# A decoder layer on one core: the low parts of the up projection's weights begin at other places in SBUF

## The chip, the cores and the metric

One core of one Trainium2 chip. The metric is the device time of one execution in microseconds, median of several runs. The kernel before takes 340.94 us (three runs, 340.84 to 341.1). Five engines work side by side on the core: TensorE (matmuls, with their weight loads as instructions of their own), VectorE, ScalarE, GpSimd and SyncE (here the issuer of all DMAs).

## The reference, cut to what matters

One hybrid decoder layer in float32 over 256 tokens of width 1024: attention and a pooling mixer side by side, gated and added to x, and then a feed-forward block. The change touches only the feed-forward block:

```python
h2 = rmsnorm(x, norm_ffn_g)
up = causal_depthwise_conv(h2 @ w_up, conv_w, conv_b)     # w_up: 1024 x 5632
gate, val = jnp.split(up, 2, axis=-1)
return x + (jax.nn.silu(gate) * val) @ w_down             # w_down: 2816 x 1024
```

## The kernel before, in words

All float32 products are made of three matmuls in the faster format float32r. Every operand is split in a high part (the value as float32r stores it) and a low part (the rest), and `mm3` adds high x high (line 94), high x low of the moving operand (line 95) and low x high (line 96). In the feed-forward block the weights are the stationary operand (128 x 128), and the activations, stored transposed, are the moving one (256 columns, all tokens). So lines 94 and 95 load the same slice of a high part, and line 96 loads the same slice of the low part.

Weights come in chunks of 128 x 2048 float32, 1 MB each, in the list `order` (lines 99 to 109): for the block, 22 up chunks and 11 down chunks, mixed. `load` (line 113) brings a chunk into one of 4 raw buffers by DMA. `next_high` (line 142) lets ScalarE write the high part into one of 4 buffers of the pool `whi`, a half chunk of 1024 columns at a time, and takes the low part's buffer from the pool `wlo` in the same breath (line 150). `next_low` (line 153) lets VectorE write raw minus high into the low buffer (line 86) and issues the next load. `ahead` runs both at places chosen by hand, so that high and low parts are ready some chunks before the matmuls need them; `chunk` (line 171) hands a chunk's two buffers to the matmuls.

One up chunk holds 1024 rows for two tiles of 128 features, one of the gate and one of the value: slices of 128 columns, 512 bytes apart per partition, 2 tiles x 8 slices (`tile_part`, line 565). So an up chunk is 48 matmuls, 16 of each line. From the fourth chunk on, each step i of the main loop (line 675) does the up tiles of chunk i and then 24 down matmuls (lines 641 to 643) for step i - 3. What else happens in a step lies on other engines: scaling and the convolution on VectorE and ScalarE, products on GpSimd. The first up tiles stand apart: between them TensorE makes the second norm's statistics (lines 242 and 253, plain float32 matmuls of another kind). After that, TensorE does nothing but up and down matmuls to the end. All instructions of one engine keep the order in which they are written (lines 709 to 715).

Where things lie in SBUF is settled by the allocator: pools follow each other in the order in which they are opened, so raw buffers, then the four of `whi`, the four of `wlo`, and behind them the activations (`act`) and temporaries. A raw, high or low buffer is 8,192 bytes in every partition, and in the program of before they all start 32 bytes past a multiple of 512. The activation tiles that are operands of the split products (`xhi`, `xlo`, `hhi`, `hlo`, `mh`, `ml`, `ath`, `poolh`, `ah`, `al` and the like) and the tiles of q and k start 480 bytes past one, with slices of 1,024 bytes; the identity matrix of the transposes starts 224 past one. Two padding lengths at the head, `HOME` and `LEAD`, set this.

Of the kernel before, what the change touches and what calls it, by code (L numbers as in the profile page):

```python
# [9 lines left out]
F32R = mybir.dt.float32r  # L10
# [4 lines left out]
P = 128  # L15
# [17 lines left out]
CH = 2048  # L33
# [21 lines left out]
FIRST = 2  # L55
HOME = 24
LEAD = 104
XCUTS = (1, 2, 3, 4, 6, 8)


@with_exitstack
def hybrid_layer_kernel(ctx: ExitStack, tc: tile.TileContext, xq_d, par_d, wkv_d, wpg_d,
# [6 lines left out]
    wlo_p = ctx.enter_context(tc.tile_pool(name="wlo", bufs=WBUFS))  # L69
# [11 lines left out]
    def high(hi, src, scale=1.0):  # L81
        nc.scalar.activation(hi, src, AF.Copy, scale=scale)  # L82
# [16 lines left out]
    order = [("q", None)] * 2 + [("k", wkv_d[c]) for c in range(2)]  # L99
# [10 lines left out]
    raws, his, los = {}, {}, {}  # L110
# [14 lines left out]
    def raw(c, sl):  # L125

        return xq[:, 4 * c + sl.start // 512, S:] if order[c][0] == "q" else raws[c][:, sl]
# [10 lines left out]
    def oldest():  # L138

        return next((c for c in range(len(order)) if c not in spent), len(order))  # L140

    def next_high():
        if at[0] < len(pieces):
            c, sl, first, _ = pieces[at[0]]
            if c - oldest() >= WBUFS:
                return
            at[0] += 1
            if first:
                his[c] = whi_p.tile([P, CH], F32R, tag="whi", name=f"hi_{order[c][0]}{c}")
                los[c] = wlo_p.tile([P, CH], F32R, tag="wlo", name=f"lo_{order[c][0]}{c}")  # L150
            high(his[c][:, sl], raw(c, sl))

    def next_low(eager=False):
# [9 lines left out]
    def ahead(upto=0):  # L163

        next_high()
        next_low()
        if at[1] - sum(p[0] < used[0] for p in pieces) < upto:
            next_high()
            next_low()
# [12 lines left out]

    xq_all = act.tile([P, LEAD + KD + KD * (S + AW)], F32, name="xq")[:, LEAD:]
    gmix = xq_all[:, 0:KD]
# [7 lines left out]
    cut = 0  # L192
    for k in XCUTS:
        end = KD + k * (S + AW)
# [28 lines left out]
    for k in range(KD):  # L223
        if k == 0:
            nc.vector.tensor_scalar(xhi[:, k, :], xT[:, k, :], gmix[:, k:k + 1], None, op0=ALU.mult)
        else:
            high(xhi[:, k, :], xT[:, k, :], gmix[:, k:k + 1])
        low(xlo[:, k, :], xhi[:, k, :], xT[:, k, :], gmix[:, k:k + 1])
        next_high()
        next_low(eager=True)  # L230
# [272 lines left out]
    for n in range(2 * KD):  # L503
# [5 lines left out]
        b, c = n // 2, n % 2  # L509
# [270 lines left out]
```

## Time and profile before

| | before |
|---|---|
| median of 3 runs | 340.94 us (340.84 to 341.1) |
| profiled execution, whole | 340.33 us |
| its span, first to last instruction | 338.6 us |
| TensorE busy, matmuls | 333.6 us (99%), 2738 matmuls |
| TensorE busy, weight loads | 323.8 us (96%) |
| VectorE, ScalarE, GpSimd busy | 259.9 (77%), 198.3 (59%), 86.4 us (26%) |
| DMA queues' share | 51.4% of 16 engines, 62.34 MB |

The views of the profile tell of one execution. Matmuls are pipelined: one takes some 0.28 us from its start to its modelled end, and the next starts long before that. So TensorE's busy time does not say how fast matmuls follow each other; the start times in the timeline do. Weight loads have rows of their own (PEld) and run beside the matmuls. "PEclk" is the share of the full TensorE clock that was granted.

### The profile page before, as it was taken

How to read it: one execution, taken by the hardware profiler on the slowest of the kernel's cores; microseconds unless marked ns; L12 is line 12 of the kernel's file. 1: busy time of each engine (PE TensorE's matmuls, PEld its weight loads, DVE VectorE, ACT ScalarE, POOL GpSimd, SP SyncE). 2: the span in 40 equal slices, each digit the busy share in tenths (PEclk: the TensorE clock that was granted, in tenths of full speed). 3: DMA queues.
4: the chain of work that ended last, by engine and by line, in shares of the span. 5: the costliest groups of instructions: out<-in, count | busy, mean ns of one | idle time of the engine just before them, and what ended most of it. 6: DMA issues, size and time to landing. Idle time of an engine off the chain costs nothing.

```text
span 338.6 us, 6730 instructions
## 1 busy us (share of the span) xinstructions
PE 333.6 (99%) x2738; PEld 323.8 (96%) x2738; DVE 259.9 (77%) x411; ACT 198.3 (59%) x319; POOL 86.4 (26%) x104
## 2 busy tenths in 40 slices
PE   8999999999999999999999999999999999999996
PEld 7888899999999999999999999999999999999995
DVE  4869989797587676798899788777777777777744
ACT  5856634635848945678366575566666665646420
POOL 1007991112203034023222322121212121212130
PEclk9999999999999999999999999999999999999999
DMA  7986562455372751466626675554646364642003
GB/s 270 417 339 240 171 222 107 156 185 206 126 271 85 248 183 71 132 251 240 250 81 197 220 250 160 215 197 178 226 149 248 126 250 137 236 149 102 0 2 124
DMA packets 10398, 62.76 MB, mean 185 GB/s; under 512 B 1152, under 2 KB 2304, under 8 KB 3456
## 3 DMA queue, kind: packets, MB, share of 16 engines
q1 hardware_dynamic: 10368, 62.34, 51.4%
q8 instruction: 21, 0.34, 0.4%
q14 instruction: 9, 0.07, 0.1%
HBM read 61.29 MB, written 1.05 MB: 184 GB/s over the span
## 4 chain that ended last, share of the span: by engine, by line
PE 97%; DMA 1%; ACT 0%; DVE 0%; issue 0%; ACTq 0%
PE ps_up L95 12%; PE ps_up L96 12%; PE ps_up L94 12%; PE ps_d L643 6%; PE ps_d L642 6%; PE ps_d L641 6%; PE ps_g L94 5%; PE ps_g L95 4%; PE ps_g L96 4%; PE ps_q L282 3%; PE ps_k L282 3%; PE ps_v L282 3%; PE ps_out L95 2%; PE ps_out L94 2%; PE ps_out L96 2%; PE ps_bp L94 1%
## 5 line engine op out<-in xcount | busy, mean ns | idle before, releaser
L94 PE MATMUL ps_up<-hhi,hi_up 128*128 128x256 f32 x352 | 97.5, 277 | 0.0
L95 PE MATMUL ps_up<-hlo,hi_up 128*128 128x256 f32 x352 | 97.3, 277 | 0.0
L96 PE MATMUL ps_up<-hhi,lo_up 128*128 128x256 f32 x352 | 97.2, 276 | 0.0
L95 PEld LDWEIGHTS ps_up<-hlo,hi_up 128*128 128x128 f32 x352 | 66.1, 188 | 0.2 <-DVE hlo L88 0.2
L94 PEld LDWEIGHTS ps_up<-hhi,hi_up 128*128 128x128 f32 x352 | 66.1, 188 | 0.0
L96 PEld LDWEIGHTS ps_up<-hhi,lo_up 128*128 128x128 f32 x352 | 66.1, 188 | 0.0
L86 DVE TENSOR_TENSOR lo_up<-raw_up,hi_up 128x1024 fp32r<-128x1024 f32 x44 | 54.8, 1247 | 6.2 <-ACT hi_up L82 6.2
L641 PE MATMUL ps_d<-ah,hi_dn 128*128 128x256 f32 x176 | 48.6, 276 | 0.0
L642 PE MATMUL ps_d<-al,hi_dn 128*128 128x256 f32 x176 | 48.6, 276 | 0.0
L643 PE MATMUL ps_d<-ah,lo_dn 128*128 128x256 f32 x176 | 48.6, 276 | 0.0
L624 POOL TENSOR_TENSOR c_v<-c_g,c_v 128x256 f32<-128x256 f32 x22 | 16.2, 737 | 118.1 <-DVE c_v L607 118.1
L82 ACT ACTIVATE hi_up<-raw_up 128x1024 fp32r<-128x1024 f32 x44 | 45.1, 1046 | 0.0
L94 PE MATMUL ps_g<-xhi,hi_g 128*128 128x256 f32 x128 | 36.4, 284 | 0.0
L82 ACT ACTIVATE ah<-c_v 128x256 fp32r<-128x256 f32 x22 | 9.2, 418 | 45.8 <-POOL c_v L624 45.8
L96 PE MATMUL ps_g<-xhi,lo_g 128*128 128x256 f32 x128 | 35.7, 279 | 0.0
L95 PE MATMUL ps_g<-xlo,hi_g 128*128 128x256 f32 x128 | 35.7, 279 | 0.0
L642 PEld LDWEIGHTS ps_d<-al,hi_dn 128*128 128x128 f32 x176 | 33.0, 188 | 0.0
L641 PEld LDWEIGHTS ps_d<-ah,hi_dn 128*128 128x128 f32 x176 | 33.0, 188 | 0.0
L643 PEld LDWEIGHTS ps_d<-ah,lo_dn 128*128 128x128 f32 x176 | 33.0, 188 | 0.0
L86 DVE TENSOR_TENSOR lo_dn<-raw_dn,hi_dn 128x1024 fp32r<-128x1024 f32 x22 | 27.3, 1242 | 0.4 <-ACT hi_dn L82 0.4
L612 DVE TENSOR_TENSOR u_v<-ps_up,R 128x256 f32<-128x256 f32 x22 | 9.3, 422 | 22.0 <-PE ps_up L96 22.0
L94 PEld LDWEIGHTS ps_g<-xhi,hi_g 128*128 128x128 f32 x128 | 24.3, 190 | 0.9 <-issue 0.5
(183 smaller groups left out, 802.3 us busy)
## 6 DMA issues: line engine op xcount, KB each, us to landing
raw_up<-in_wup SPq DMA_DIRECT2D x22, 1024.0 KB, 4.8
raw_dn<-in_wdn SPq DMA_DIRECT2D x11, 1024.0 KB, 4.8
raw_g<-in_wpg SPq DMA_DIRECT2D x8, 1024.0 KB, 4.8
raw_o<-in_wout SPq DMA_DIRECT2D x4, 1024.0 KB, 4.9
raw_v<-in_wkv SPq DMA_DIRECT2D x2, 1024.0 KB, 13.6
raw_p<-in_wpg SPq DMA_DIRECT2D x2, 1024.0 KB, 6.2
raw_bp<-in_wbp SPq DMA_DIRECT2D x2, 1024.0 KB, 4.9
raw_ba<-in_wba SPq DMA_DIRECT2D x2, 1024.0 KB, 4.8
```

The source lines that it names most:

```text
L82: nc.scalar.activation(hi, src, AF.Copy, scale=scale)
L86: nc.vector.tensor_tensor(lo, src, hi.bitcast(F32), ALU.subtract)
L94: nc.tensor.matmul(out, sh, mh, start=start, stop=False, **kw)
L95: nc.tensor.matmul(out, sh, ml, start=False, stop=False, **kw)
L96: nc.tensor.matmul(out, sl, mh, start=False, stop=stop, **kw)
L282: nc.tensor.matmul(pt[t], sx[:, k, t * P:(t + 1) * P], wx[:, sl], start=k == 0 and sx is xhi and wx is hi, stop=k == KD - 1 and wx is lo)
L612: nc.vector.tensor_tensor(u, ps[:, 0:S], R2, ALU.mult)
L624: nc.gpsimd.tensor_tensor(uc[1], g[1], uc[1], ALU.mult)
L641: nc.tensor.matmul(o, hi[:, sl], acch[i], start=first, stop=False, skip_group_check=True)
L642: nc.tensor.matmul(o, hi[:, sl], accl[i], start=False, stop=False, skip_group_check=True)
L643: nc.tensor.matmul(o, lo[:, sl], acch[i], start=False, stop=i == KF - 1, skip_group_check=True)
```

## The change

The four buffers of the pool `wlo` get 128 more columns (512 bytes). The low part of a chunk still fills 2048 columns, but for the up chunks it begins at a place that a table gives: up chunk n begins 16 x `LOWS[n]` columns, 64 x `LOWS[n]` bytes, behind the buffer's start. For all other chunks, and for up chunks whose entry is 0, it begins at the start as before. The list `at_up` in the new line counts the up chunks that stand ahead in `order`. All readers and writers of the low part get the shifted view, so that nothing else is edited.

```diff
+LOWS = (0, 0, 4, 4, 0, 2, 2, 0, 1, 1, 0, 6, 6, 0, 3, 3, 0, 5, 5, 0, 7, 7)
...
                 his[c] = whi_p.tile([P, CH], F32R, tag="whi", name=f"hi_{order[c][0]}{c}")
-                los[c] = wlo_p.tile([P, CH], F32R, tag="wlo", name=f"lo_{order[c][0]}{c}")
+                at_up = [i for i in range(c) if order[i][0] == "up"]
+                place = 16 * LOWS[len(at_up)] if order[c][0] == "up" else 0
+                los[c] = wlo_p.tile([P, CH + P], F32R, tag="wlo", name=f"lo_{order[c][0]}{c}")[:, place:]
             high(his[c][:, sl], raw(c, sl))
```

## Rows read from the trace of the kernel before

**Rows 1.** The page: busy time by engine, and the chain that ended last.
```profile
PE 333.6 (99%) x2738; PEld 323.8 (96%) x2738; DVE 259.9 (77%) x411; ACT 198.3 (59%) x319; POOL 86.4 (26%) x104
...
PE 97%; DMA 1%; ACT 0%; DVE 0%; issue 0%; ACTq 0%
```

**Rows 2.** Stretches: length, busy us (instructions) by engine, PEclk, DMA share, GB/s.
```profile
131.60:154.30 22.70, 22.70 (x196) 22.70 (x195) 17.29 (x25) 15.24 (x25) 5.46 (x8) 1.00 0.50 170
...
163.60:324.30 160.70, 160.70 (x1418) 160.67 (x1417) 124.34 (x187) 94.70 (x142) 35.87 (x42) 1.00 0.50 176
```

**Rows 3.** Timeline of TensorE: start us, duration us; four starts.
```profile
131.68 0.28 PE L94 MATMUL ps_out<-mh,hi_o 128*128 128x256 f32 x1
...
154.29 0.28 PE L94 MATMUL ps_up<-hhi,hi_up 128*128 128x256 f32 x1
...
180.15 0.28 PE L94 MATMUL ps_up<-hhi,hi_up 128*128 128x256 f32 x1
...
188.31 0.28 PE L94 MATMUL ps_up<-hhi,hi_up 128*128 128x256 f32 x1
```

**Rows 4.** Matmuls by line: count, duration ns min/median/max, first and last start.
```profile
L94 PE MATMUL ps_out<-mh,hi_o x64: 281/281/281, 131.7 to 153.9; 128*128 128x256 f32 x64
...
L95 PE MATMUL ps_up<-hlo,hi_up x10: 278/281/281, 160.0 to 163.1; 128*128 128x256 f32 x10
...
L94 PE MATMUL ps_up<-hhi,hi_up x328: 276/276/473, 163.6 to 324.0; 128*128 128x256 f32 x164
...
L641 PE MATMUL ps_d<-ah,hi_dn x176: 276/276/276, 177.4 to 334.9; 128*128 128x256 f32 x176
```

**Rows 5.** Timeline of TensorE at two disturbances, and line 95 between them.
```profile
156.41 0.28 PE L94 MATMUL ps_up<-hhi,hi_up 128*128 128x256 f32 x1
156.66 0.39 PE L95 MATMUL ps_up<-hlo,hi_up 128*128 128x256 f32 x1
...
L95 PE MATMUL ps_up<-hlo,hi_up x7: 276/276/279, 157.1 to 159.2; 128*128 128x256 f32 x7
...
163.38 0.60 PE L253 MATMUL ps_n<-diag,ones 128*128 128x256 f32 x2
163.62 0.47 PE L94 MATMUL ps_up<-hhi,hi_up 128*128 128x256 f32 x1
163.93 0.28 PE L95 MATMUL ps_up<-hlo,hi_up 128*128 128x256 f32 x1
164.05 0.28 PE L96 MATMUL ps_up<-hhi,lo_up 128*128 128x256 f32 x1
164.17 0.28 PE L94 MATMUL ps_up<-hhi,hi_up 128*128 128x256 f32 x1
```

**Rows 6.** Line 95 behind three of the 15 entries, columns as in rows 4.
```profile
L95 PE MATMUL ps_u<-xlo,hi_p x16: 276/276/280, 39.5 to 44.6; 128*128 128x256 f32 x16
...
L95 PE MATMUL ps_u<-xlo,hi_p x16: 281/281/281, 45.8 to 51.1; 128*128 128x256 f32 x16
...
L95 PE MATMUL ps_bp<-pooll,hi_bp x8: 281/281/281, 117.7 to 120.1; 128*128 128x256 f32 x8
```

**Rows 7.** Low parts from 163.6 us; a weight load in the timeline; the stage's waits.
```profile
L86 DVE TENSOR_TENSOR lo_up<-raw_up,hi_up x37: 1215/1224/1714, 162.7 to 311.0; 128x1024 fp32r<-128x1024 f32 x37
...
180.15 0.19 PEld L95 LDWEIGHTS ps_up<-hlo,hi_up 128*128 128x128 f32 x1
...
DVE u_v L612 <- PE ps_up L96: 22.0, 16, 1.7
```

**Rows 8.** Timeline of TensorE in the q projection, 512 columns; 18 matmuls apart.
```profile
11.89 0.39 PE L282 MATMUL ps_q<-lo_q,xhi 128*128 128x512 f32 x1
...
16.01 0.39 PE L282 MATMUL ps_q<-lo_q,xhi 128*128 128x512 f32 x1
```

**Rows 9.** The transposes of k: timeline, and durations of one.
```profile
54.18 1.03 PE L318 MATMUL ps_tk<-ident,qg_k 128*128 128x128 f32 x8
...
L318 PE MATMUL ps_tk<-ident,qg_k x8: 271/272/273, 54.2 to 54.9; 128*128 128x128 f32 x8
```

## The prediction, made before the change was run

> **What bounds the kernel now.** I read the page first: TensorE is busy for 333.6 us of a span of 338.6, and the chain that ended last is TensorE for 97% [rows 1]. VectorE, the next one, is at 77%. So the question for any edit here is what it does to the pace of TensorE's matmuls, and nothing else is near the path.
>
> Then the stretches of the kernel by engine [rows 2]. [...] A "busy" of 100% hides the pace, because matmuls overlap. The pace is the distance from one start to the next, and that is read from the timeline [rows 3]: between 131.68 and 154.29 us lie 192 matmuls of the output projection, 22.61 us, so 117.76 ns each; between 180.15 and 188.31 lie 72 matmuls, one whole step of up (48) and down (24), 8.16 us, so 113.33 ns each. Same shape, 128x128 weights against 256 columns, same clock, 4.43 ns apart. The duration of one matmul tells the two paces apart in the grouped views too [rows 4]: median 281 ns at the slow pace, 276 at the fast one. By that mark the up matmuls after 163.6 us, 3 x 328, and all 528 down matmuls run fast, the first of them apart; the output projection and the up matmuls from 160.0 to 163.1 run slow.
>
> The reader should see one thing more: the pace is not fixed by the operands. The same line, reading the same kind of buffers at the same distances, runs at either pace. What changes it is a disturbance of the stream [rows 5]: the matmul behind the one at 156.41 us had to wait and started 0.25 us later, and the stream that had been slow came out fast (line 95 from 157.1 to 159.2: median 276 ns); at 163.38 two matmuls of another kind cut into a slow stream, then starts follow at 0.31, 0.12 and 0.12 us, and it is fast. Between disturbances a pace is kept: the slow one through the whole output projection, the fast one for 171 us to the end. I count 15 entries into this kind of stream behind a block of other matmuls or a wait, from 39.4 to 163.6 us; 8 came out fast, 7 slow (the first two and one of the late slow ones stand in [rows 6]).
>
> **The change part by part.** No instruction is added, removed or moved, no wait either. Four buffers grow from 8,192 to 8,704 bytes. That moves what lies behind them by 2,048 bytes, a multiple of 512, so all operands but the low parts keep their places modulo 512; the buffers' own growth is 512 each. Between the two column halves of one up chunk the weights differ by 512 bytes already, and the pace is 113.33 over both in the step of [rows 3], so I put 512 at nothing. If it cost something it would do so at the slow pace's 4.43 ns.
>
> What is left is the low part of 14 of the 22 up chunks: chunks 2, 3, 5, 6, 8, 9, 11, 12, 14, 15, 17, 18, 20 and 21 begin 64 to 448 bytes further on. Call distance the start of the weights minus the start of the moving operand, modulo 512. Today it is 64 for all matmuls of the stage. In a triple of lines 94, 95, 96 it stays 64 for two, and the third gets 320, 192, 128, 448, 256, 384 and 0, two chunks each.
>
> VectorE writes these low parts (line 86, median 1,224 ns, worst 1,714 [rows 7]). If all 28 shifted ones took the worst time, 28 x 0.490 = 13.7 us more, this would go into VectorE's idle 160.7 - 124.3 = 36.4 us of the stage [rows 2]. What hides it is that VectorE works chunks ahead: it waits for up matmuls 22.0 us in 16 waits, and the waits of the stage name no matmul that waits for anything [rows 7]. So nothing; without this cover the 13.7 us would be in the sum.
>
> For TensorE no row shows the new distances with this shape. Nearest rows: at 113.33 the load of a matmul's weights starts with the matmul before it [rows 7], so weights are read while the moving operand of another matmul is, and I read the two paces as two ways in which these reads fall against each other. Distance 448 occurs with 512 columns in the q projection, weights from x and moving from the weight buffer: 18 matmuls from 11.89 to 16.01 us, 229 ns each, 114.4 per 256 columns [rows 8], between the paces. Distance 256 occurs in the transposes of k: eight take 1.03 us with the last one's 0.27, so 109 ns each [rows 9], but with 128 columns and another data path. Bounds for one shifted matmul: +4.43 ns and -4.3 ns.
>
> Now the sums, against the profiled execution, 340.33 us with a span of 338.6. Lows alone at the slow pace: 14 x 16 x 4.43 ns = 0.99 us. All matmuls of the shifted chunks: 14 x 48 x 4.43 = 2.98. If the stream is thrown to the slow pace at the first border and stays, as the slow pace stayed through [rows 3]: 20 chunks x 48 + 22 x 24 = 1,488 matmuls, 6.6 us. If nothing: 0. The sequence has 13 borders between one shift and another. I take each as a disturbance that can land either way, as 7 of 15 did, and count half of the 14 shifted steps as slow with their down matmuls: 7 x 72 x 4.43 ns = 2.23 us. That gives 342.56 for the profiled execution. The median of the three runs shown is 0.61 above the profiled one, so 343.2 us.
>
> **The rivals.** *No change.* The pace could be a matter of timing between the two streams alone and not of addresses. For it: both paces occur at one and the same distance, and the fast one passes from up to down and back at every step, with other moving tiles, without a ripple [rows 3, 4]. Against it: those tiles all sit at the same distance, so the trace never tried another. Price: 0, 340.9 us. [...]
>
> *Faster.* Some distances could read better than today's. For it: the 109 ns of the transposes. If the shifted lows went from 113.33 to 109, 14 x 16 x 4.33 ns = 0.97 us would go, 340.0; if they drew their whole triples along, 2.9 us, 338.0. Against it: in the fast pace up and down run at the same 113.33 without a trace of variation, which looks like a floor of this shape. It decides from the first shifted chunk, about 166 us.
>
> *Slower and stuck.* The same mechanism as my forecast, but no border restores the fast pace, since no matmul of another kind comes after 163.6: 6.6 us, 347.5. It decides at the first border, chunk 2.
>
> **How the numbers follow.** Slower by over 0.2% (0.68 us, about what a measurement of this kernel can tell from no change): 0.47, of which 0.05 for stuck; within 0.2%: 0.38, which holds the case of lows alone at fewer than 10 chunks; faster: 0.15. Likeliest is slower, at 343.2. Its own range is 341.7 to 347. For 8 in 10 the range takes in no change and leaves out most of the faster case and the stuck end: 340.2 to 346.8.
>
> **What would show it.** Forecast right: the up matmuls of some shifted chunks have a median of 281 ns or more and steps of about 8.48 us in place of 8.16, with TensorE still busy all the time and no new wait. If lows alone pay, only the start behind line 96 or ahead of it is late. No change: steps of 8.16 throughout. Faster: steps under 8.16 in the shifted chunks. I am wrong in kind if the time moves outside 166 to 335 us, if a wait on line 86 shows up ahead of TensorE, or if the first two chunks change.

## The result, and the profile after

| | before | after |
|---|---|---|
| median of 3 runs | 340.94 us (340.84 to 341.1) | 343.44 us (343.41 to 343.62) |
| profiled execution, whole | 340.33 us | 343.62 us |
| its span | 338.6 us | 341.8 us |
| TensorE busy, matmuls | 333.6 us | 337.5 us |

The ratio of the two is 1.0074, 95% interval 1.0051 to 1.0097: slower, by 2.5 us, and the interval leaves out no change. The forecast was 343.2.

The page of after, busy time and chain, answers to [rows 1]: the same instructions, TensorE as full as before, and nothing else moved up.

```profile
PE 337.5 (99%) x2738; PEld 327.7 (96%) x2738; DVE 259.6 (76%) x411; ACT 198.2 (58%) x319; POOL 87.4 (26%) x104
...
PE 98%; ACT 0%; DVE 0%; issue 0%; ACTq 0%
```

The waits of after from 164 us to the end, the longest and the one that answers to the wait of [rows 7] (who waited for whom, us in total, times, longest). No matmul waits for anything here either:

```profile
POOL c_v L628 <- DVE c_v L611: 119.8, 22, 6.9
...
DVE u_v L616 <- PE ps_up L98: 23.8, 16, 2.1
```

So the 3.2 us of span went into TensorE's matmuls, and nearly all of it into matmuls that follow each other more slowly. The change adds lines at the top: lines 94, 95, 96 of before are 96, 97, 98 of after, the down matmuls are 645 to 647. In the timeline of TensorE in after, the first matmul of a chunk marks the step. These are the starts of chunks 7 to 10 and 14 to 21, and answer to the last two of [rows 3]:

```profile
204.93 0.28 PE L96 MATMUL ps_up<-hhi,hi_up 128*128 128x256 f32 x1
213.09 0.28 PE L96 MATMUL ps_up<-hhi,hi_up 128*128 128x256 f32 x1
221.49 0.28 PE L96 MATMUL ps_up<-hhi,hi_up 128*128 128x256 f32 x1
229.89 0.28 PE L96 MATMUL ps_up<-hhi,hi_up 128*128 128x256 f32 x1
...
262.53 0.28 PE L96 MATMUL ps_up<-hhi,hi_up 128*128 128x256 f32 x1
271.00 0.28 PE L96 MATMUL ps_up<-hhi,hi_up 128*128 128x256 f32 x1
279.48 0.28 PE L96 MATMUL ps_up<-hhi,hi_up 128*128 128x256 f32 x1
287.96 0.28 PE L96 MATMUL ps_up<-hhi,hi_up 128*128 128x256 f32 x1
296.47 0.28 PE L96 MATMUL ps_up<-hhi,hi_up 128*128 128x256 f32 x1
304.87 0.28 PE L96 MATMUL ps_up<-hhi,hi_up 128*128 128x256 f32 x1
313.02 0.28 PE L96 MATMUL ps_up<-hhi,hi_up 128*128 128x256 f32 x1
321.50 0.28 PE L96 MATMUL ps_up<-hhi,hi_up 128*128 128x256 f32 x1
```

A fast step is 8.16 us. Chunk 7 has it, and so have chunks 10 to 13: 262.53 - 229.89 = 32.64 us, four steps. The others against it:

| chunk | shift, x 64 bytes | step, us | over 8.16 |
|---|---|---|---|
| 2, 3, 5, 6, 11, 12 | 4, 4, 2, 2, 6, 6 | 8.16 where a whole step stands | 0 |
| 8, 9 | 1, 1 | 8.40, 8.40 | 0.48 |
| 14, 15 | 3, 3 | 8.47, 8.48 | 0.63 |
| 16 | 0 | 8.48 | 0.32 |
| 17, 18 | 5, 5 | 8.51, 8.40 | 0.59 (0.35 and 0.24) |
| 19 | 0 | 8.15 | 0 |
| 20 | 7 | 8.48 | 0.32 |

Behind the start of chunk 21 stand 143 more matmuls, 4.4 ns each over the fast pace, 0.6 us. That is 3.0 us, and together with 0.3 that the profiled execution was late at chunk 4 already (180.45 in place of 180.15 us) it is the whole difference of the two profiled executions, 3.29 us. Of this 0.3, 0.2 was there when the k projection began, at 16.70 in place of 16.47. The rest lies in chunk 0, which isn't shifted: the wait of [rows 5] stands in after too, but here the stream came out of it slow.

```profile
156.88 0.39 PE L97 MATMUL ps_up<-hlo,hi_up 128*128 128x256 f32 x1
...
L97 PE MATMUL ps_up<-hlo,hi_up x7: 277/281/281, 157.3 to 159.5; 128*128 128x256 f32 x7
```

Two things are to be seen. Only odd shifts cost anything; the distance is 64 x (1 + shift), so an odd shift makes it a multiple of 128. And they cost in two ways: behind shift 1, and behind the second chunk of shift 5, the stream is fast again, while the chunk behind 3 stays slow though its own shift is 0. Shift 5 met a stream that was slow already, and the down matmuls behind its first chunk, 17, were still slow. The durations of matmuls by line, behind chunks 8, 14, in 16, and behind 18 (columns as in [rows 4]), show it: the down matmuls behind chunk 8 are fast again, behind chunk 14 they stay slow, chunk 16 runs slow at shift 0, and behind chunk 18 the stream has come back.

```profile
L646 PE MATMUL ps_d<-al,hi_dn x6: 276/276/276, 219.2 to 220.9; 128*128 128x256 f32 x6
...
L646 PE MATMUL ps_d<-al,hi_dn x6: 281/281/281, 268.6 to 270.4; 128*128 128x256 f32 x6
...
L97 PE MATMUL ps_up<-hlo,hi_up x14: 281/281/281, 280.0 to 284.5; 128*128 128x256 f32 x14
...
L646 PE MATMUL ps_d<-al,hi_dn x6: 276/276/276, 302.6 to 304.3; 128*128 128x256 f32 x6
```

### The profile page after: what moved, and what is told of

It is laid out like the page before. It is cut to its first block, busy times and chain, and to the rows that moved or that the text cites. A ratio compares the mean times of both kernels' runs of the same rounds, so it can differ in the third digit from the quotient of the medians.

```text
span 341.8 us, 6730 instructions
## 1 busy us (share of the span) xinstructions
PE 337.5 (99%) x2738; PEld 327.7 (96%) x2738; DVE 259.6 (76%) x411; ACT 198.2 (58%) x319; POOL 87.4 (26%) x104
## 4 chain that ended last, share of the span: by engine, by line
PE 98%; ACT 0%; DVE 0%; issue 0%; ACTq 0%
PE ps_up L96 12%; PE ps_up L97 12%; PE ps_up L98 12%; PE ps_d L645 6%; PE ps_d L647 6%; PE ps_d L646 6%; PE ps_g L96 5%; PE ps_g L97 4%; PE ps_g L98 4%; PE ps_q L286 3%; PE ps_k L286 3%; PE ps_v L286 3%; PE ps_out L97 2%; PE ps_out L98 2%; PE ps_out L96 2%; PE ps_warm L210 1%
```

## The experiments

Each starts from the changed kernel (lines 96 to 98 and 645 to 647) unless said otherwise; where an edit adds or takes away lines, the same matmuls have other numbers. The kernel before, run beside them, took 340.50, 340.56 and 340.53 us in the three groups of runs.

**1. Even shifts alone.** My forecast took every border between two shifts as a disturbance that may land either way. The step table speaks for another rule, parity: odd shifts cost, even ones don't.

```diff
-LOWS = (0, 0, 4, 4, 0, 2, 2, 0, 1, 1, 0, 6, 6, 0, 3, 3, 0, 5, 5, 0, 7, 7)
+LOWS = (0, 0, 4, 4, 0, 2, 2, 0, 0, 0, 0, 6, 6, 0, 0, 0, 0, 0, 0, 0, 0, 0)
```

> The changed kernel with only its even shifts kept (chunks 2, 3, 5, 6, 11, 12 by 4, 2 and 6 times 64 bytes), the odd ones set to 0. Theory 'parity': only odd multiples of 64 bytes cost anything; every step stays at 8.16 us and the time is that of before, 340.9 us, within 0.2 us. Rival 'border', the one on which the prediction rests: each border between one shift and another throws the stream to a pace by chance; half of 6 shifted steps slow, 3 x 0.32 = 0.96 us, about 341.9 us, with more if a slow pace stays. Rival 'where the stream stands': the slow steps come at a time of the stage whatever the shifts, and the steps from 262 us on stay slow: about 343.

Measured: 340.68 us, ratio 1.0003 (0.9993 to 1.0012). The matmuls of line 97 and of the down projection, by line:

```profile
L97 PE MATMUL ps_up<-hlo,hi_up x327: 276/276/276, 164.6 to 324.4; 128*128 128x256 f32 x164
...
L646 PE MATMUL ps_d<-al,hi_dn x176: 276/276/276, 177.9 to 335.3; 128*128 128x256 f32 x176
```

Minimum, median and maximum are 276 ns: six borders between shifts, and not one matmul of these lines left the fast pace. The theory that any border disturbs falls, and so does a slow time of the stage. The run also shows that the larger buffers by themselves cost nothing that it can tell: 340.68 us against 340.50.

**2. Shift 1 for all chunks.**

```diff
+LOWS = (1,) * 22
```

> All 22 up chunks with their low part 64 bytes on (shift 1). Theory 'parity': shift 1 forces a slow up stage at 118.0 ns as in chunks 8 and 9 of the changed kernel, and down goes back to 113.3 within some matmuls: 0.24 us more in each of about 20.5 steps behind 163.6 us, 4.9 us in all, 345.8 us (5.0 more at most). Rival 'border': with no border left there is no disturbance, and the stage runs at one pace: 340.9, or 347.5 if it enters slow.

Measured: 345.41 us, ratio 1.0141 (1.0126 to 1.0156), 4.9 us over before. By line:

```profile
L97 PE MATMUL ps_up<-hlo,hi_up x272: 278/282/283, 181.3 to 321.0; 128*128 128x256 f32 x136
...
L646 PE MATMUL ps_d<-al,hi_dn x175: 276/276/281, 178.4 to 339.9; 128*128 128x256 f32 x175
```

No matmul of line 97 comes under 278 and the down median is 276: at shift 1 every chunk is slow and the down matmuls between recover, as the theory says, 0.24 us a step. The first whole step, which the stream entered slow, is the exception: there the down matmuls stayed slow too (8.50 us; the maximum of 281 ns above).

**3. Shift 3 once.** Only chunk 8, everything else at 0.

```diff
+LOWS = (0,) * 8 + (3,) + (0,) * 13
```

> Only chunk 8 is shifted, by 3 times 64 bytes; all other low parts lie as in the kernel before. Theory 'throws and stays': a distance that is a multiple of 256 throws the stream to the slow pace, which then keeps itself though all later distances are 64: 1,080 matmuls from chunk 8 to the end at 4.43 ns, 4.8 us, about 345.7 us. Rival 'the pace follows the operands in use': only chunk 8 is slow, 48 x 4.4 = 0.2 us: 341.1 us.

Measured: 345.34 us, ratio 1.0138 (1.0121 to 1.0155), 4.84 us over before, where "throws and stays" had 4.8. The low part of one chunk, placed 192 bytes further on, slows some 1,080 matmuls, all but 16 of which read nothing that was moved. The timeline at the border (chunk 8 begins at 212.98):

```profile
212.86 0.28 PE L647 MATMUL ps_d<-ah,lo_dn 128*128 128x256 f32 x1
212.98 0.28 PE L96 MATMUL ps_up<-hhi,hi_up 128*128 128x256 f32 x1
213.09 0.28 PE L97 MATMUL ps_up<-hlo,hi_up 128*128 128x256 f32 x1
213.20 0.28 PE L98 MATMUL ps_up<-hhi,lo_up 128*128 128x256 f32 x1
213.32 0.28 PE L96 MATMUL ps_up<-hhi,hi_up 128*128 128x256 f32 x1
213.44 0.28 PE L97 MATMUL ps_up<-hlo,hi_up 128*128 128x256 f32 x1
```

Up to the first matmul on a moved low part (213.20) three steps take 0.34 us, 0.113 each; behind it two take 0.24, 0.12 each. The down matmuls of that run, from 218.7 us to the end, never come back:

```profile
L646 PE MATMUL ps_d<-al,hi_dn x130: 280/282/282, 218.7 to 337.8; 128*128 128x256 f32 x130
```

**4. Which two operands.** Four runs ask what the distance is a distance between. In all of them the up chunks have shift 1. They rest on when the weights are loaded. In the timeline of before (matmuls, then weight loads) the load of line 96 begins with the matmul of line 95, on hlo, and that of a chunk's first weights with the last down matmul, on ah, 0.12 us behind the start of one on al:

```profile
179.92 0.28 PE L642 MATMUL ps_d<-al,hi_dn 128*128 128x256 f32 x1
180.04 0.28 PE L643 MATMUL ps_d<-ah,lo_dn 128*128 128x256 f32 x1
...
180.26 0.28 PE L95 MATMUL ps_up<-hlo,hi_up 128*128 128x256 f32 x1
...
180.04 0.19 PEld L94 LDWEIGHTS ps_up<-hhi,hi_up 128*128 128x128 f32 x1
...
180.27 0.19 PEld L96 LDWEIGHTS ps_up<-hhi,lo_up 128*128 128x128 f32 x1
```

First hlo moves along (xlo, whose buffer it takes, gets the same size and stays), so that the low weights stand at 64 again to the operand that streams while they are loaded:

```diff
+LOWS = (1,) * 22
...
-    hlo = act.tile([P, KD, S], F32R, tag="xlo", name="hlo")
+    hlo = act.tile([P, KD * S + P], F32R, tag="xlo", name="hlo")[:, 16:16 + KD * S].rearrange("p (k s) -> p k s", s=S)
```

> As the kernel with shift 1 for all up chunks, and the low part of the moving operand, hlo, is placed 64 bytes further on as well. Theory 'the load and the stream beside it': what counts is the distance between the weights being loaded and the moving operand that streams at that moment. The low weights of line 96 are loaded while line 95 streams hlo, so with both moved their distance is 64 again, and all other pairs are as before: every step 8.16 us, 340.9 us. Rival 'a matmul's own operands': the distance of a matmul's weights to its own moving operand counts. Then line 95 gets 0 and line 96 gets 128, both multiples of 128, and the stage is slow: 345.8 us or more. Rival 'high against low weights': the distance of the low part to the high part counts, which is 64 here: 345.8.

Measured: 345.76 us, ratio 1.0153 (1.0138 to 1.0168). The theory of the one operand streaming beside the load falls. Line 97:

```profile
L97 PE MATMUL ps_up<-hlo,hi_up x272: 279/281/282, 181.2 to 321.1; 128*128 128x256 f32 x136
```

Then the high weights move along instead:

```diff
-                his[c] = whi_p.tile([P, CH], F32R, tag="whi", name=f"hi_{order[c][0]}{c}")
...
+                his[c] = whi_p.tile([P, CH + P], F32R, tag="whi", name=f"hi_{order[c][0]}{c}")[:, place:]
```

> High and low parts of all up chunks 64 bytes on, so that low against high is 0 as in the kernel before, and all weights stand at distance 128 to the moving operands. Theory 'distance to the moving operand': slow, at least as with the low parts alone (345.4 us); if each of the three loads of a triple pays the 14 ns that one paid there, 127 ns for a matmul and some 355 us. Rival 'high against low weights': fast, 340.6 us.

Measured: 345.96 us, ratio 1.0162 (1.0146 to 1.0178). Low against high is as in the kernel before, and it is slow all the same, so that the distance between the two weights isn't it. Nor does each load pay by itself: with low parts alone a triple is some 14 ns longer (0.24 us over 16 triples), and three loads at distance 128 cost hardly more than one. Two starts of its timeline, one step of 8.43 us, against 8.40 with the low parts alone:

```profile
189.40 0.28 PE L96 MATMUL ps_up<-hhi,hi_up 128*128 128x256 f32 x1
...
197.83 0.28 PE L96 MATMUL ps_up<-hhi,hi_up 128*128 128x256 f32 x1
```

Then all four move, high and low weights, hhi and hlo (the edits above, and the same for hhi). All distances within the up stage are 64 again; only at the borders between up and down do they differ.

> High and low weights of all up chunks and both parts of the moving operand (hhi, hlo) 64 bytes on: all distances 64 as before, all places odd where they were even. Theory 'distance': every up step back at 8.16 us, 340.6 us. Rival 'place of the weights by itself': as slow as with both weights moved alone, 345.4 us or more.

Measured: 344.95 us, ratio 1.0128 (1.0112 to 1.0144). By its time this looks like the rival, and the trace says otherwise. From 164.8 to the first down matmul the stream is fast, on weights that all lie at the "odd" places (by line):

```profile
L97 PE MATMUL ps_up<-hlo,hi_up x39: 276/276/276, 164.8 to 177.7; 128*128 128x256 f32 x39
```

Then comes the first border (timeline):

```profile
177.74 0.28 PE L97 MATMUL ps_up<-hlo,hi_up 128*128 128x256 f32 x1
177.85 0.28 PE L98 MATMUL ps_up<-hhi,lo_up 128*128 128x256 f32 x1
177.97 0.28 PE L645 MATMUL ps_d<-ah,hi_dn 128*128 128x256 f32 x1
178.08 0.28 PE L646 MATMUL ps_d<-al,hi_dn 128*128 128x256 f32 x1
178.20 0.28 PE L647 MATMUL ps_d<-ah,lo_dn 128*128 128x256 f32 x1
178.32 0.28 PE L645 MATMUL ps_d<-ah,hi_dn 128*128 128x256 f32 x1
```

Up to the first down matmul (177.97) two steps take 0.23 us; the three behind it take 0.35, 0.117 each, and the down matmuls of this step are slow. Its own operands are both unmoved, at 64; but its weights, if loads lie here as in the timeline of before, were loaded while the moved hhi streamed, at distance 0. So the place of the weights by itself is ruled out, and so is a rule on a matmul's own operands alone: an operand of a neighbouring matmul has part in it. That their reads meet is my estimate; no row shows a read. From there on the borders set the pace, both ways. In the later steps the up chunk is slow from its start, though all its distances are 64 (chunk 5, below): at the border its first weights, by the same timeline, were loaded while the unmoved al or ah streamed, at distance 128. And behind the slow chunk 5 the down matmuls come back to the fast pace over the border at distance 0.

```profile
L97 PE MATMUL ps_up<-hlo,hi_up x15: 281/281/281, 189.3 to 194.3; 128*128 128x256 f32 x15
...
L646 PE MATMUL ps_d<-al,hi_dn x7: 276/276/276, 195.3 to 197.4; 128*128 128x256 f32 x7
```

So it is not a rule for every arrangement that 128 slows only while it lasts and that 0 throws.

Last, the triple in another order (high x high, low x high, high x low), for the up matmuls alone, with low weights and hlo moved:

```diff
+                nc.tensor.matmul(ps[:, 0:S], hi[:, sl], oph[:, k, :], start=k == 0, stop=False)
+                nc.tensor.matmul(ps[:, 0:S], lo[:, sl], oph[:, k, :], start=False, stop=False)
+                nc.tensor.matmul(ps[:, 0:S], hi[:, sl], opl[:, k, :], start=False, stop=k == KD - 1)
```

> Low weights and hlo 64 bytes on in the up stage, as in the run that stayed slow at 118.3 ns, but with the triple in another order: high x high, low weights x high, high weights x low. Theory 'weights are read while the matmul two ahead streams': the low weights are then read beside hlo (distance 64), the high ones beside hhi (64): every step 8.16 us, 340.6 us. Rival 'a matmul's own two operands' and rival 'the matmul one ahead': distances of 0 and 128 stay among the pairs, so slow, 345.4 to 346.

Measured: 347.74 us, ratio 1.0213 (1.0197 to 1.0229): slow again, and here the down matmuls stay slow too, from the second whole step on (line 651 here). The second of the triple, on low weights, and the down matmuls:

```profile
L576 PE MATMUL ps_up<-hhi,lo_up x272: 278/282/286, 181.5 to 323.1; 128*128 128x256 f32 x136
...
L651 PE MATMUL ps_d<-al,hi_dn x162: 281/281/282, 187.2 to 340.8; 128*128 128x256 f32 x162
```

So the operand two matmuls ahead isn't the whole rule either. Three moving operands are candidates for what the distance of a matmul's weights is counted to: its own, the one of the matmul ahead and the one two ahead. None of them alone fits all four runs, any two together do. No run parts these pairs, and none tests the distance between hhi and hlo by itself, which the first and the last of the four changed as well: which operands count stays open, and why they do no run shows.

**5. The slow pace broken ahead of the block.** In [rows 3] the output projection runs slow, and behind shift 1 the stream came back in after (down matmuls behind chunk 8: 276 ns). Here no up chunk is shifted, but five chunks that ran slow, wholly or in part, before the feed-forward block.

```diff
+LOWS = (0,) * 22
+RESET = (7, 11, 14, 16, 18)
...
-                place = 16 * LOWS[len(at_up)] if order[c][0] == "up" else 0
+                place = 16 * (c in RESET)
```

> No up chunk shifted; instead the low parts of five chunks ahead of the feed-forward block lie 64 bytes on: the second p chunk, the g chunks of outputs 6 and 7, 10 and 11, 14 and 15, and the second bp chunk. Each stands where the stream of before runs slow, wholly or for its second half. Theory 'shift 1 breaks the slow pace': behind each of them the stream comes out fast and stays fast to the next block of another kind; 24 + 24 + 24 + 24 + 280 matmuls gained net, x 4.43 ns = 1.7 us, about 338.9 us. Rival 'the slow pace returns at distance 64': no gain, up to 72 + 24 matmuls lost, 340.6 to 341.

Measured: 340.01 us, ratio 0.9987 (0.9977 to 0.9996): 0.55 us faster, a third of what was expected. (Lines 97 to 99 are the triple in this and the next kernel.) The theory holds for three of the five: behind entries 7, 11 and 18 of `order` the stream came out fast, behind 14 and 16 it did not. The last one frees the whole output projection (by line), and the up projection starts at 153.08 in place of 154.29 us:

```profile
L98 PE MATMUL ps_out<-ml,hi_o x64: 276/276/276, 131.4 to 152.9; 128*128 128x256 f32 x64
```

More than half of the gain of 1.21 us is given back there. The waits of TensorE now have a row that before did not:

```profile
PE ps_up L98 <- DVE hlo L91: 0.7, 1, 0.7
```

The up projection's operands are ready when VectorE has written them, and here a stream that arrived 1.21 us sooner waited 0.7 us for them.

The same with the two that failed left out:

```diff
+RESET = (7, 11, 18)
```

> The run with five shifted chunks ahead of the feed-forward block gained 0.55 us; two of its five did not bring the stream back to the fast pace and cost 24 matmuls each. Here only the three that did are left: the second p chunk, the g chunk of outputs 6 and 7, the second bp chunk. Theory: 2 x 24 x 4.43 ns + 2 x 0.05 = 0.3 us less than with five: 339.7 us, 0.8 us below before; the rest of the gain ahead of the up projection is eaten there, where the stream waits for hhi and hlo. Rival: the entries behind come out otherwise, and the gain is anything from 0 to 1.5 us.

Measured: 340.14 us over 11 runs, ratio 0.9983 (0.9974 to 0.9992): no better than with five, where 339.7 was expected. Its trace shows how a gain of this kind can be lost, in one execution: at 340.39 us it was slower than most of the eleven, while the trace of the run with five shifted chunks is that of its fastest. The output projection is entered fast, and two microseconds later one weight load comes 0.1 us late, and so does the matmul behind it (timeline of the matmuls, then of a write by VectorE and of the late load, then the rest of the projection by line):

```profile
133.73 0.28 PE L97 MATMUL ps_out<-mh,hi_o 128*128 128x256 f32 x1
133.85 0.38 PE L98 MATMUL ps_out<-ml,hi_o 128*128 128x256 f32 x1
134.06 0.28 PE L99 MATMUL ps_out<-mh,lo_o 128*128 128x256 f32 x1
...
133.38 0.41 DVE L89 TENSOR_TENSOR ml<-xq,mh 128x256 fp32r<-128x256 f32 x1
133.84 0.19 PEld L98 LDWEIGHTS ps_out<-ml,hi_o 128*128 128x128 f32 x1
...
L98 PE MATMUL ps_out<-ml,hi_o x57: 281/281/281, 134.3 to 154.1; 128*128 128x256 f32 x57
```

From 134.06 on the stream is slow and stays so through the projection. The late load begins 0.05 us after VectorE has written the moving operand's low part (133.38 + 0.41 = 133.79); in the run with five shifted chunks the same write ended at 133.31. So this too looks like a stream that arrived sooner than its operand, though the views name no wait there. Both versions beat the kernel before, by 0.13 and 0.17%.

**6. Other distances for all weights.** From the kernel before, with all weight buffers moved against the activations, to distance 192 and to 96.

```diff
-HOME = 24
+HOME = 56
...
-LEAD = 104
+LEAD = 72
```

> The kernel before with all weight buffers 128 bytes further on, the activations at their places: distance 192 in place of 64 for every split product. Theory 'odd multiples of 64 bytes are alike': the fast pace exists and keeps itself as before; a slow pace exists too, and which entry comes out slow may change: 340.5 us if the feed-forward block is entered fast, up to 347 if slow. Rival 'at 192 the slow pace does not hold': all stretches that ran slow ahead of 163 us, some 670 matmuls, run fast, and up to 3.0 us go: 337.6 to 339.

Measured: 349.04 us, ratio 1.0248 (1.0234 to 1.0263). At 192 both paces exist, the first theory's case: eight triples of the gates run at 276 ns, but the feed-forward block is entered slow and stays so, one step 8.49 us. The slow mark here is 279 ns. By line:

```profile
L95 PE MATMUL ps_g<-xlo,hi_g x8: 276/276/276, 103.0 to 105.4; 128*128 128x256 f32 x8
...
L95 PE MATMUL ps_up<-hlo,hi_up x325: 279/279/279, 167.0 to 332.4; 128*128 128x256 f32 x163
```

And two starts a step apart in its timeline:

```profile
182.79 0.28 PE L94 MATMUL ps_up<-hhi,hi_up 128*128 128x256 f32 x1
...
191.28 0.28 PE L94 MATMUL ps_up<-hhi,hi_up 128*128 128x256 f32 x1
```

The time is over the 347 expected at most; the first of the two starts lies 2.64 us behind the one at 180.15 in [rows 3], so the stretches ahead took longer as well. With `HOME = 32` and `LEAD = 96`, distance 96:

> The kernel before with all weight buffers 32 bytes further on, the activations at their places: distance 96, half way between 64 (fast pace possible) and 128 (no fast pace seen). Theory 'blocks of 64 bytes': reads of one block fall partly on the next, so the fast pace does not hold, and the up and down stage runs near 118 ns: 345 to 348 us. Rival 'only distances near a multiple of 128 cost': as before, 340.5 us.

Measured: 349.96 us, ratio 1.0258 (1.0225 to 1.029). That is over the 345 to 348 of the first theory as well; one of the four runs took 347.78. No matmul of line 95 in the block is at 276, and the up projection begins at 155.69 in place of 154.29 us, so the stretches ahead are slower too. That a block of 64 bytes has part in it was an estimate; no run shows one:

```profile
L95 PE MATMUL ps_up<-hlo,hi_up x324: 277/281/283, 166.9 to 333.1; 128*128 128x256 f32 x162
```

## Why the prediction was right, and which of its steps was not

**The bound.** Right. TensorE had work all the time before and after (busy 99% in both), the cost is in the pace, no wait came up ahead of it, and the writing of the shifted low parts (line 86) is no term.

**512 bytes at nothing.** Right: experiment 1 has the larger buffers and 340.68 us, against 340.50 beside it.

**The mechanism, a stream with two paces that the change throws.** Right, and stronger than I had put it: experiment 3 throws the stream with the first moved low part and it stays thrown to the end (line 646 at 282 ns from 218.7 to 337.8 us).

**The term "half of the 14 shifted steps slow, as 7 of 15 entries".** Near in size, wrong in reason, and that it came near is luck. I took each border for a disturbance by chance. Experiment 1 has six borders and none throws. Nor were the 15 entries tosses. In the traces of before and after the 12 entries up to 117.7 us come out the same way both times: the four behind the attention's score products (`ps_s`) fast (line 95, in after 97, at a median of 276 ns), the four behind its value products (`ps_o`) slow (281). What decides in the block is the distance: at 192, 320 and 448 (even shifts) the fast pace goes on (276 ns throughout in experiment 1); at 128 (shift 1, 8.40 us a step) the chunk is slow and the stream returns behind it, and at 384 (shift 5) a slow stream returned behind the second chunk (8.51, then 8.40); at 256 and 0 (shifts 3, 7, both 8.48) it is thrown and stays. That 8 of 14 shifted chunks are slow is the count of odd numbers in the table, not the count of a coin.

**The price of a slow step, 72 x 4.43 ns = 0.32 us with its down matmuls.** Right where the stream stays thrown: 0.31 and 0.32 for chunks 14 to 16 and 20. For shift 1 and chunk 18 it is 0.24, since the down matmuls recover; that is some 5 ns for each of 48 up matmuls, over my bound of 4.43. Chunk 17, where they don't, costs 0.35. Not reckoned were a chunk at 0 that stays slow (16, 0.32 us) and the 143 matmuls behind the start of chunk 21 (0.6). 7 x 0.32 = 2.23 was forecast, 3.0 is in the trace and 3.29 between the profiled executions; the medians differ by 2.5, since the profiled execution of before was 0.61 us below its median and that of after 0.18 above. So 343.2 against 343.44 owes much to misses that cancel. With 3 at chunk 2 and neither 1 nor 5 behind it, the "stuck" rival's 6.6 us would be the estimate (experiment 3, from chunk 8 on, has 4.84); that table was not run.

**Where the time moves.** I called it wrong in kind if the time moved outside 166 to 335 us or the first two chunks changed. In the profiled executions 0.3 us did move ahead of 166, of it 0.1 in chunk 0. It isn't the shifts' doing: chunk 0 has none, and experiment 1, with the same larger buffers, took 340.68 us.

**Where lows alone would show.** I named the start behind the low matmul or ahead of it. At shift 1 the whole triple is drawn along (experiment 2: line 97, on high weights, has a median of 282).

**The rivals.** "No change" fails with experiments 2 and 3: shift 1 in all chunks cost 4.9 us, and moving the low weights of one chunk by 192 bytes cost 4.84 us. "Faster" found nothing: no distance tried ran under the 113.33 ns of [rows 3] (the shortest step in the table above is 8.15 us, 113.2 ns a matmul); that it is the floor of this shape stays my estimate. The 109 ns of the transposes at distance 256, 0.85 ns for each of 128 columns where the block has 0.44 for each of 256, told nothing of it, since 256 is one of the two distances that throw. "Stuck" is the mechanism of shifts 3 and 7; the slow stretch behind shift 3 ended in after with the two chunks of shift 5.

## What to carry to other kernels

Where TensorE is busy all the time, read the distance between starts, stretch by stretch; a busy share of 100% hid 4% here. When two stretches of equal shape differ, look for what came ahead of the slow one, a wait, a block of another kind, operands placed otherwise, because in these runs the stream kept a pace that it was once thrown into (4.84 us behind one chunk in experiment 3). Before moving operands in SBUF, try the places in one run, as this change did, with a few chunks each and a plain chunk between, and tell what a place costs while it lasts from what stays behind it.

## What the runs showed of the hardware that I had not expected

Each line tells what was measured when buffers of this program were moved. What inside the chip makes the difference, no run shows.

- Split-float32 matmuls (128x128 weights, 256 columns) run at 113.33 ns or near 118 ns from start to start ([rows 3]), at a granted clock of 1.00 in both, and in the block the pace went with the weights' place against the moving operands' place. Of the multiples of 64 bytes that were tried for the low weights, 64, 192, 320 and 448 had 276 ns throughout in experiment 1, and the chunks with 128 (8.40 us a step), 256 and 0 (both 8.48) and 384 (8.51 and 8.40) ran slow, where a fast step is 8.16. At 96 for all weights no matmul of line 95 in the block is fast (277 at least, median 281).
- For the low weights alone, 256 (8.48 us a step) and 0 (8.48) throw a fast stream to a slow pace that stays when the place is mended (256: 4.84 us from one chunk); 128 slows it while it lasts (0.24 us a step). A slow stream came back behind 384 (after two chunks of shift 5: 281 ns, then 276), and behind 128 in three of five places in experiment 5 (the last of them: 276 ns through the output projection, 281 in before). With other operands moved as well it goes otherwise: in experiment 4 a chunk of 48 matmuls at distance 64 ran slow behind a border at 128 (281 ns), and behind a border at 0 the stream was fast again (276).
- A place at which the fast pace was seen does not by itself make it: with all weights at 192 the block ran slow to the end, at 279 ns and 349.04 us.
- A delay of 0.1 us ahead of one matmul was followed by a change of pace for the next 170 (experiment 5, second run: 276 ns before, 281 behind). The wait of [rows 5] was followed by the other change in before (281, then 276), and in after the stream was slow behind it (281): how a wait of this length lands is not settled by these runs.
